# Later silu, later second halves of the streams, single-bank decays and another end of `up` in a two-layer trunk

## The chip, the cores and the metric

One core of one Trainium2 chip runs the whole program in one launch. The time is the device time of one execution in microseconds (us). Three executions of the kernel before took 2153.89, 2152.57 and 2152.16 us; their median is 2152.57.

## The reference

Two residual layers over 1024 tokens of width 1024, all in float32. Layer 0 mixes tokens with a gated MLP and with windowed attention; layer 1 with chunked gated linear attention (GLA). Each layer ends in a gated MLP with a causal convolution of width 3. The parts that the change touches:

```python
def gla_mixer(h, w_in, w_a2, b_a, head_g, w_out):
    z = h @ w_in
    q, k, v, r, ga = jnp.split(z, [hk, 2 * hk, 2 * hk + hv, 2 * hk + 2 * hv], axis=-1)
    log_a = jax.nn.log_sigmoid((ga @ w_a2 + b_a).astype(jnp.float32)) / C_TAU
    o = gla_chunked(heads(q, C_DK) * (C_DK ** -0.5), heads(k, C_DK), heads(v, C_DV), heads(log_a, C_DK))
    o = rms_norm(o, head_g)
    o = o.transpose(0, 2, 1, 3).reshape(Bn, S, hv) * jax.nn.silu(r.astype(jnp.float32))
    return o.astype(h.dtype) @ w_out

def conv_ffn(h, w_gate, w_up, conv_w, conv_b, w_down):
    g = causal_dwconv(h @ w_gate, conv_w, conv_b)
    return (jax.nn.silu(g) * (h @ w_up)) @ w_down
```

There are 4 GLA heads with 128 query and key columns and 256 value columns each; the MLP is 2816 wide.

## The kernel before

**Products.** TensorE multiplies float32 in a reduced form. So each operand is split into a high part (ScalarE's copy, line 100, a CAST in the profile) and a low part (VectorE's difference, line 101), and each product is three passes, `PASSES`: high x high, high x low, low x high. The third pass needs the low part of the weights.

**Streams.** The large products go by Strassen's scheme with seven half-size products instead of eight. A *stream* makes two 128-column blocks of an output for all 1024 tokens. Its `step(p)` splits the weights of product p (a raw quarter of the weights, or a sum of quarters: S5, S6, S7, S3), issues 12 matmuls of 128x512 (4 blocks x 3 passes) into a PSUM bank and then empties the bank or adds it to an output. Three banks serve a stream: A for product 2, C for 5 and 3, B for 1, 6, 7 and 4. Bank B is emptied between two products: 1 and 6 and 4 by a copy on ScalarE, 7 in the GLA by an addition on VectorE (`V.tensor_add(C22, C22, o)`, line 1063), in the MLP by a copy on ScalarE and an addition from there. C collects two products: the second is added to an output after both.

**GLA** (function `gla`). After the values (`values`, banks `pv`) come eight streams, q0 r0 q1 r1 ... r3: `q{h}` makes query and key of head h, `r{h}` its gate, which silu (line 1168) turns in place and which is stored to `rsd` for the first three heads. After each q comes `core(h)`: eight chunks of 128 tokens with small matmuls (`pat`, `pog`), then `decays(h + 1)`: two matmuls `pla`, then |x|, exp and ln on ScalarE (lines 1082 to 1085, two tables of functions), a difference on VectorE (line 1086), eight scans on VectorE (line 1089), a difference on GpSimd (line 1094) and exponentials. The first decays are made within `values`, in a wide slot (two banks) of the pool `mm`.

**Raw weights and sums.** A stream's two raw halves (`rq`, `rr`) come by DMA from SyncE's queue into four buffers; its sums have two buffers.

**The MLP.** `ffn_up` runs 22 streams, gate and up in turn (g0, u0, ... g20, u20), with bank names `pgA`, `puB` and so on; `ffn_down` comes after u20.

**What sets the order.** The kernel is written without waits: a scheduler with a timeline model of its own arranges each engine's instructions from the program and puts the waits in. Each engine takes its own queue in order. `tc.keep_in_program_order(ins)` holds an instruction at its place in the program; `tc.issue_after(ins)`, used by the change alone, makes VectorE's instructions that are written in the block come after `ins` on VectorE. PSUM has eight banks; after the values they are five for the tag `m1` and three for `pt`.

Of the kernel before, what the change touches and what calls it, by code (L numbers as in the profile page):

```python
# [55 lines left out]
def trunk(ctx: ExitStack, tc: tile.TileContext, a, out):  # L56
# [181 lines left out]
    def ffn_up(l, T3, ps, pool, norm_end):  # L238
# [6 lines left out]
        def stream(kind, f):  # L245

            raws = [load_raw(w_of(kind)[l, f + i], f"r{kind}{f + i}") for i in range(2 if f else 1)]
            A11, A12, A21, A22 = (raws[i][:, c] if f or not i else None for i in range(2) for _, c in HALVES)
            out = pool.tile([P, 2, S], F32, tag=kind, bufs=1, name=f"{kind}{f}")
            (C11, C12), (C21, C22) = ([out[:, i, c] for _, c in HALVES] for i in range(2))  # L250
            s1 = pool.tile([P, 512], F32, tag="s1", bufs=2, name=f"s1{kind}{f}")
            sums, bank, made = {}, {}, {}

            def summed(name, x, y, op):
                sums[name] = pool.tile([P, 512], F32, tag="S", bufs=4, name=f"{name}{kind}{f}")
                G.tensor_tensor(sums[name], x, y, op=op)  # L256
# [12 lines left out]

            def prep(p):  # L270
                if f == 0 and p > 2:
                    w = wp.tile([P, 2, 512], F32R, tag="w", name=f"w{kind}{f}p{p}")
                    Q.dma_start(f32(w), sided[l][kind, p])
                    made[p] = [w[:, i, :] for i in range(2)]
                else:
                    made[p] = parts_of(left(p), f"w{kind}{f}p{p}")

            def step(p):
                if p not in made:
                    prep(p)  # L280
                L = made[p]

                b = {2: "A", 5: "C", 3: "C"}.get(p, "B")
                more = b in bank
                if not more:
                    bank[b] = ps.tile([P, 512], F32, tag="pt" if b == "A" else "m1", name=f"p{kind}{b}{f}")
                o = bank[b]
                for j in range(4):
                    for ii, jj in PASSES:
                        T.matmul(o, L[ii][:, j * P : j * P + P], right[p][:, jj, j, :], skip_group_check=more,  # L290
                                 start=(not more and j == 0 and (ii, jj) == PASSES[0]),
                                 stop=(j == 3 and (ii, jj) == PASSES[-1]))
                if p == 1:
                    A.copy(s1, o)
                elif p == 2:
                    V.tensor_add(C11, s1, o)
                elif p == 6:
                    A.copy(C12, o)
                elif p == 5:
                    A.copy(C22, o)  # L300
                elif p == 7:
                    A.copy(s1, o)  # L302
                    V.tensor_add(C22, C22, s1)  # L303
                elif p == 4:
                    A.copy(C21, o)  # L305
                elif p == 3:
                    V.tensor_add(C12, C12, o)

            return step, out, prep
# [50 lines left out]
        for i, (kind, f) in enumerate(todo):  # L360
# [5 lines left out]
            if 0 < i < len(todo) - 1:  # L366
                nxt = stream(*todo[i + 1])
                nxt[0](1)
            step(4)
            step(3)  # L370
            if kind == "g":
                ts = conv(f, out)
            else:
# [524 lines left out]
    def gla(ps, narrow, gl, T3, rl):  # L898
# [43 lines left out]
        def values():  # L942

            for i, (col, step, w) in enumerate(((0, 272, 1), (256, 256, 2), (512, 512, 1))):
# [6 lines left out]
                for m in sorted(range(NT // (2 * w)), key=lambda m: 2 * w * m < 4):  # L951
# [26 lines left out]
                    if (i, m) == (1, 1):  # L978
                        decay_input()
                    if (i, m) == (2, 2):  # L980
                        first = decays(0, "mm")
            return first

        def minus(o, t, x, y):
# [32 lines left out]
        def stream(name, src, pool, **tag):  # L1017
# [24 lines left out]
            def step(p):  # L1042
# [17 lines left out]
                elif p == 5:  # L1060
                    A.copy(C22, o)
                elif p == 7:
                    V.tensor_add(C22, C22, o)
                elif p == 4:
                    A.copy(C21, o)
                elif p == 3:
                    V.tensor_add(C12, C12, o)
# [73 lines left out]
                return stream(f"q{h}", [a["w_qk"][2 * h + i] for i in range(2)], gl, tag="out", bufs=1)  # L1141
            return stream(f"r{h}", [a["w_r"][2 * h + i] for i in range(2)], rl, tag="r")

        cur = begin(*todo[0])
        cur[0](1)
        for i, (kind, h) in enumerate(todo):
            step, out = cur
            for p in (5, 6, 2, 7) if i + 1 < len(todo) else (6, 2, 7):
                step(p)
            if i + 1 < len(todo):  # L1150
                nxt = begin(*todo[i + 1])
                nxt[0](1)
            step(4)
            step(3)
            if i + 2 == len(todo):
                nxt[0](5)
            if kind == "q":
# [5 lines left out]
                core(h, out[:, 0, :], out[:, 1, :], dec)  # L1163
                if h + 1 < HEADS_C:
                    dc = decays(h + 1)
            else:
                for _, c in HALVES:
                    A.activation(out[:, :, c], out[:, :, c], AF.Silu)
                if h + 1 < HEADS_C:
                    Q.dma_start(rsd[:, 2 * h : 2 * h + 2, :], out)  # L1170
                else:
                    return ps, out
            cur = nxt


# [8 lines left out]

    def narrow():
        pss.close()
        return banks(pss, m1=5, pt=3)

    a_cat = even(gm_open)
    Q.dma_start(hg, a["head_g"])  # L1190
# [155 lines left out]
```

## Time and profile before

| of the profiled execution | |
|---|---|
| time of the execution | 2153.94 us |
| span from first to last instruction | 2152.2 us |
| TensorE (PE) busy | 2125.0 us, 99% |
| TensorE's weight loads (PEld) | 1801.6 us, 84% |
| VectorE (DVE) | 1528.2 us, 71% |
| ScalarE (ACT) | 1034.8 us, 48% |
| GpSimd (POOL) | 490.5 us, 23% |
| DMA queue of SyncE (q1), share of 16 engines | 48.3% |
| TensorE's idle time by waits, the longest | pj 5.9, po 2.2 in three, pBq 2.1 in two, pj 2.1, pv 1.6 us |

A row of the timeline gives the start in us from the span's beginning, the time from start to end, engine, line, operation, `out<-in`, shapes, and the count of equal instructions in the row; in square brackets the idle time of that engine just before it and what ended it. PE is TensorE's matmul, PEld its weight load, SPq the queue of DMAs. Names in the profile lose their last number (`pBq` is bank B of any q stream); `or` and `oq` are the outputs of r and q streams, `wq1p` the split weights of q1.

### The profile page before, as it was taken

The page shows a single profiled execution, that of the slowest core. Times are in us where ns is not written, and L with a number is a line of the kernel's source. Part 1 is how long each engine was busy: PE and PEld are TensorE (multiplying, and loading weights), DVE is VectorE, ACT ScalarE, POOL GpSimd, SP SyncE. Part 2 cuts the span into 40 slices and gives each one's busy share as a digit, 9 for nine tenths or more (in the row PEclk, how much of TensorE's full clock was granted, in tenths as well). Part 3 has the DMA queues.
Part 4 walks back from the last instruction along what each step waited for, and adds up shares of the span by engine and source line. Part 5 has one row for each costly group of instructions (what it writes and reads, how often), then busy time and mean ns, then how long its engine had stood idle before and what let it go on. Part 6 is the DMA issues. An engine that isn't in the chain of part 4 may idle for free.

```text
span 2152.2 us, 29720 instructions
## 1 busy us (share of the span) xinstructions
PE 2125.0 (99%) x10444; PEld 1801.6 (84%) x10444; DVE 1528.2 (71%) x2451; ACT 1034.8 (48%) x1998; POOL 490.5 (23%) x521
## 2 busy tenths in 40 slices
PE   8999999999999999999999999999999999999999
PEld 7999988888888888888898888878788888888887
DVE  7566655587878889655577777677778888785554
ACT  7555664264444444444454455535544444444443
POOL 6444310013424334000010011011234334220000
PEclk9999999999999999999999999999999999999999
DMA  7122313754444544765553233486554444457664
GB/s 273 33 68 68 104 43 115 262 196 156 153 164 154 174 154 150 258 230 198 208 179 108 79 106 100 138 291 213 176 166 161 166 154 155 162 181 280 214 216 165
DMA packets 159413, 353.70 MB, mean 164 GB/s; under 512 B 17392, under 2 KB 54256, under 8 KB 158880
## 3 DMA queue, kind: packets, MB, share of 16 engines
q1 hardware_dynamic: 159264, 351.81, 48.3%
q8 instruction: 82, 1.34, 0.3%
q14 instruction: 67, 0.55, 0.1%
HBM read 243.15 MB, written 108.59 MB: 163 GB/s over the span
## 4 chain that ended last, share of the span: by engine, by line
PE 91%; DVE 3%; DMA 2%; ACT 2%; issue 1%; SPq 0%; POOL 0%; DVEq 0%; ACTq 0%
PE puB L290 11%; PE pgB L290 11%; PE po L190 7%; PE pv L190 6%; PE pj L190 6%; PE pgC L290 6%; PE puC L290 6%; PE pdB L397 5%; PE pdC L397 5%; PE pdO L397 4%; PE puA L290 3%; PE pgA L290 3%; PE pdP L397 2%; PE pdQ L397 2%; PE pu L190 2%; PE pBq L1051 2%
## 5 line engine op out<-in xcount | busy, mean ns | idle before, releaser
L101 DVE TENSOR_TENSOR da<-ar,da 128x512 fp32r<-128x512 f32 x154 | 106.1, 689 | 154.7 <-ACT da L100 154.6
L100 ACT CAST da<-ar 128x512 fp32r<-128x512 f32 x154 | 95.9, 623 | 206.7 <-PE pdC L397 99.6
L190 PE MATMUL po<-wo,hq 128*128 128x512 f32 x768 | 184.6, 395 | 2.3 <-ACT hq L100 2.2
L190 PEld LDWEIGHTS po<-wo,hq 128*128 128x128 f32 x768 | 141.5, 188 | 32.6 <-ACT hq L100 2.9
L190 PE MATMUL pv<-wv,hq 128*128 128x512 f32 (+2 forms) x768 | 140.8, 340 | 1.6 <-DVE b L1083 1.6
L397 PE MATMUL pdB<-dw,da 128*128 128x512 f32 x528 | 135.5, 391 | 0.9 <-ACT u L305 0.7
L397 PE MATMUL pdC<-dw,da 128*128 128x512 f32 x528 | 135.1, 390 | 0.0
L190 PEld LDWEIGHTS pv<-wv,hq 128*128 128x128 f32 x768 | 118.7, 189 | 16.4 <-DVE b L1083 2.1
L397 PEld LDWEIGHTS pdB<-dw,da 128*128 128x128 f32 x528 | 98.7, 188 | 22.4 <-ACT u L305 1.1
L256 POOL TENSOR_TENSOR S1g<-rg 128x512 f32<-128x512 f32 x20 | 30.0, 1501 | 381.9 <-DMA wsd<-D 322.6
L397 PEld LDWEIGHTS pdC<-dw,da 128*128 128x128 f32 x528 | 99.0, 188 | 20.5
L101 DVE TENSOR_TENSOR dw<-wr,dw 128x512 fp32r<-128x512 f32 x154 | 105.7, 686 | 11.1 <-ACT dw L100 11.0
L140 POOL TENSOR_SCALAR rn<-ssq 128x1 f32<-128x1 f32 x24 | 9.7, 403 | 450.0 <-ACT h L148 245.1
L190 PE MATMUL pj<-wq,hq 128*128 128x384 f32 x576 | 110.2, 339 | 0.0
L100 ACT CAST dw<-wr 128x512 fp32r<-128x512 f32 x154 | 95.0, 617 | 16.2 <-DMA wr<-in_w_dn 9.3
L397 PE MATMUL pdO<-dw,da 128*128 128x512 f32 x396 | 102.2, 389 | 0.2 <-DVE dw L101 0.2
L190 PEld LDWEIGHTS pj<-wq,hq 128*128 128x128 f32 x576 | 99.1, 188 | 0.0
L397 PEld LDWEIGHTS pdO<-dw,da 128*128 128x128 f32 x396 | 74.3, 188 | 16.0 <-DVE dw L101 0.6
L319 DVE SCALAR_TENSOR_TENSOR t<-g,cw,t 128x1022 f32<-128x1022 f32 x44 | 76.6, 1742 | 0.1
L318 DVE SCALAR_TENSOR_TENSOR t<-g,cw,t 128x1023 f32<-128x1023 f32 x44 | 58.8, 1337 | 16.4 <-ACT t L317 16.4
L303 DVE TENSOR_TENSOR g<-g,s1g 128x512 f32<-128x512 f32 x22 | 15.2, 691 | 76.9 <-ACT s1g L302 76.9
L320 ACT ACTIVATE t<-t 128x1024 f32<-128x1024 f32 x44 | 46.7, 1062 | 32.2 <-DVE t L319 32.2
(1080 smaller groups left out, 5438.9 us busy)
## 6 DMA issues: line engine op xcount, KB each, us to landing
ar<-actd SPq DMA_DIRECT2D x70, 512.0 KB, 3.5
rd<-in_w_down SPq DMA_DIRECT2D x44, 512.0 KB, 3.6
wsd<-D SPq DMA_DIRECT2D x88, 256.0 KB, 2.2
rg<-in_w_gate SPq DMA_DIRECT2D x42, 512.0 KB, 3.7
ru<-in_w_up SPq DMA_DIRECT2D x42, 512.0 KB, 4.6
wr<-wsd SPq DMA_DIRECT2D x40, 512.0 KB, 4.4
actd<-t SPq DMA_DIRECT2D x66, 256.0 KB, 2.2
wr<-in_w_dn SPq DMA_DIRECT2D x30, 512.0 KB, 4.8
```

Source lines behind the costliest of these rows:

```text
L100: (hi or A.copy)(dst[0], src)
L101: (lo or V.tensor_sub)(dst[1], src, f32(dst[0]))
L140: G.tensor_scalar(r, ssq, 1.0 / n, EPS, op0=ALU.mult, op1=ALU.add)
L190: T.matmul(o, L[i], R[jj][:, sl], start=(k == 0 and (ii, jj) == PASSES[0]), stop=(k == nk - 1 and (ii, jj) == PASSES[-1]))
L256: G.tensor_tensor(sums[name], x, y, op=op)
L290: T.matmul(o, L[ii][:, j * P : j * P + P], right[p][:, jj, j, :], skip_group_check=more, start=(not more and j == 0 and (ii, jj) == PASSES ...
L303: V.tensor_add(C22, C22, s1)
L318: V.scalar_tensor_tensor(t[:, 1:], g[:, : S - 1], w(1), t[:, 1:], op0=ALU.mult, op1=ALU.add)
L319: V.scalar_tensor_tensor(t[:, 2:], g[:, : S - 2], w(0), t[:, 2:], op0=ALU.mult, op1=ALU.add)
L320: A.activation(t, t, AF.Silu)
L397: T.matmul(o, L[ii][:, t * P : t * P + P], R[jj], skip_group_check=more, start=start and not more and (ii, jj) == PASSES[0], stop=stop and ...
L1051: T.matmul(o, L[ii][:, j * P : j * P + P], right[p][:, jj, j, :], skip_group_check=more, start=(not more and j == 0 and (ii, jj) == PASSES ...
```

## The change

Five edits:

- In `ffn_up` the first and the last stream (g0, u20), in both layers, end with products 7, 3, 4 instead of 7, 4, 3. The first matmul of 3 is held there.
- The first decays are put into single banks (tag `pt`) instead of a slot of the wide pool.
- In the GLA the steps 4 and 3 of every stream are written under `issue_after` of product 7's addition: on VectorE their low parts, the sum S3 and the additions come behind it.
- Silu of `r{h}` and its store are written after product 6 of the next q stream instead of after the r stream, and held in the order of the program. For the last head they stay.
- `narrow()` opens the pool of `pt` ahead of that of `m1`, so that `pt` has other banks.

```diff
@@ ffn_up, step
-            def step(p):
+            def step(p, pin=False):
...
-                        T.matmul(o, L[ii][:, j * P : j * P + P], right[p][:, jj, j, :], skip_group_check=more,
...
+                        mm = T.matmul(o, L[ii][:, j * P : j * P + P], right[p][:, jj, j, :], skip_group_check=more,
...
+                        if pin and j == 0 and (ii, jj) == PASSES[0]:
+                            tc.keep_in_program_order(mm)
@@ ffn_up, the loop over streams
             if 0 < i < len(todo) - 1:
                 nxt = stream(*todo[i + 1])
                 nxt[0](1)
-            step(4)
-            step(3)
+                step(4)
+                step(3)
+            else:
+                step(3, pin=True)
+                step(4)
@@ gla, values
                     if (i, m) == (2, 2):
-                        first = decays(0, "mm")
+                        first = decays(0, "pt")
@@ gla, step
                 elif p == 7:
-                    V.tensor_add(C22, C22, o)
+                    return V.tensor_add(C22, C22, o)
@@ gla, the loop over streams
+        def gates(h, out):
+            for _, c in HALVES:
+                tc.keep_in_program_order(A.activation(out[:, :, c], out[:, :, c], AF.Silu))
+            if h + 1 < HEADS_C:
+                Q.dma_start(rsd[:, 2 * h : 2 * h + 2, :], out)
+
-        cur = begin(*todo[0])
+        cur, pending = begin(*todo[0]), None
...
             for p in (5, 6, 2, 7) if i + 1 < len(todo) else (6, 2, 7):
-                step(p)
+                added = step(p)
+                if p == 6 and pending:
+                    gates(*pending)
+                    pending = None
...
-            step(4)
-            step(3)
+            with tc.issue_after(added.ins):
+                step(4)
+                step(3)
...
+            elif h + 1 < HEADS_C:
+                pending = h, out
             else:
-                for _, c in HALVES:
-                    A.activation(out[:, :, c], out[:, :, c], AF.Silu)
-                if h + 1 < HEADS_C:
-                    Q.dma_start(rsd[:, 2 * h : 2 * h + 2, :], out)
-                else:
-                    return ps, out
+                gates(h, out)
+                return ps, out
@@ narrow
-        return banks(pss, m1=5, pt=3)
+        return banks(pss, pt=3, m1=5)
```

How the instructions stand on the engines, at three places. Here the names keep their numbers: `pBq0` is bank B of stream q0, `wq0p7` the weights of its product 7.

TensorE, from product 2 of q0 to the start of `core(0)`. Before:

```order
L1051 MATMUL pBq0_11606<-Tm1_10706,wq0p6_11641 128x512 x12
L1051 MATMUL pAq0_11660<-hq10_87,wq0p2_11657 128x512 x2
L1051 MATMUL pBr0_11701<-hq00_85,wr0p1_11698 128x512 x12
L1051 MATMUL pCq0_11625<-hq11_88,wq0p3_11733 128x512 x8
L1051 MATMUL pBq0_11606<-Tm2_10707,wq0p7_11676 128x512 x12
L1051 MATMUL pCq0_11625<-hq11_88,wq0p3_11733 128x512 x4
L1051 MATMUL pBr0_11701<-Tm1_10706,wr0p6_11978 128x512 x12
L1051 MATMUL pBq0_11606<-hq01_86,wq0p4_11715 128x512 x12
L1051 MATMUL pBr0_11701<-Tm2_10707,wr0p7_12013 128x512 x12
L1107 MATMUL pat00_11755<-oq0_11601 128x128
```

After:

```order
L1056 MATMUL pBq0_11606<-Tm1_10706,wq0p6_11641 128x512 x12
L1056 MATMUL pAq0_11660<-hq10_87,wq0p2_11657 128x512 x2
L1056 MATMUL pBr0_11701<-hq00_85,wr0p1_11698 128x512 x12
L1056 MATMUL pBq0_11606<-Tm2_10707,wq0p7_11676 128x512 x12
L1056 MATMUL pBq0_11606<-hq01_86,wq0p4_11715 128x512 x12
L1056 MATMUL pCq0_11625<-hq11_88,wq0p3_11733 128x512 x12
L1056 MATMUL pBr0_11701<-Tm1_10706,wr0p6_11978 128x512 x2
L1112 MATMUL pat00_11755<-oq0_11601 128x128
```

Between 7 and 4 of q0 stood `pCq0` and product 6 of r0; now 4 follows 7 without anything between, then 3, then two matmuls of r0's product 6.

TensorE, from the decays of head 1 (`pla10`, `pla11`) on, after `core(0)`. Before:

```order
L1079 MATMUL pla10_11931<-gaT_10730,wa2_10715 128x512
L1079 MATMUL pla11_11935<-gaT_10730,wa2_10715 128x512
L1051 MATMUL pAq1_12129<-hq10_87,wq1p2_12126 128x512
L1051 MATMUL pCr0_11962<-Tm0_10705,wr0p5_11959 128x512 x12
L1051 MATMUL pBq1_12038<-hq00_85,wq1p1_12035 128x512 x12
L1051 MATMUL pCq1_12094<-Tm0_10705,wq1p5_12091 128x512 x12
L1051 MATMUL pBr1_12170<-hq00_85,wr1p1_12167 128x512 x2
L1051 MATMUL pCr0_11962<-hq11_88,wr0p3_12070 128x512 x7
L1051 MATMUL pBr0_11701<-hq01_86,wr0p4_12052 128x512 x12
L1051 MATMUL pCr0_11962<-hq11_88,wr0p3_12070 128x512 x5
L1051 MATMUL pBq1_12038<-Tm1_10706,wq1p6_12110 128x512 x12
```

After:

```order
L1084 MATMUL pla10_11931<-gaT_10730,wa2_10715 128x512
L1084 MATMUL pla11_11935<-gaT_10730,wa2_10715 128x512
L1056 MATMUL pCr0_11962<-Tm0_10705,wr0p5_11959 128x512 x12
L1056 MATMUL pBq1_12038<-hq00_85,wq1p1_12035 128x512 x12
L1056 MATMUL pBr0_11701<-hq01_86,wr0p4_12052 128x512 x12
L1056 MATMUL pCr0_11962<-hq11_88,wr0p3_12070 128x512 x12
L1056 MATMUL pCq1_12091<-Tm0_10705,wq1p5_12088 128x512 x2
L1056 MATMUL pBq1_12038<-Tm1_10706,wq1p6_12107 128x512
L1056 MATMUL pCq1_12091<-Tm0_10705,wq1p5_12088 128x512 x10
L1056 MATMUL pBq1_12038<-Tm1_10706,wq1p6_12107 128x512
L1056 MATMUL pAq1_12129<-hq10_87,wq1p2_12126 128x512 x2
```

Products 4 and 3 of r0 now stand ahead of products 5, 6 and 2 of q1; before, 2 and 5 of q1 and a part of r1's 1 stood ahead of them.

VectorE at the same place, from the difference of the decays (`g11`) on. Before (product 4's and 3's low parts of r0 stand further up, ahead of `pla`):

```order
L1086 TENSOR_TENSOR g11_11929<-b1_11930,g11_11929 128x1024
L1063 TENSOR_TENSOR or0_11696<-or0_11696,pBr0_11701 128x512
L101 TENSOR_TENSOR wq1p4_12184<-rq11_12031,wq1p4_12184 128x512
L1089 SCALAR_TENSOR_TENSOR b1_11930<-one_10718,g11_11929 128x128 x8
L1057 TENSOR_TENSOR oq1_12033<-s1q1_12034,pAq1_12129 128x512
L101 TENSOR_TENSOR wq1p3_12202<-S3q1_12200,wq1p3_12202 128x512
L1091 TENSOR_TENSOR dec1_11950<-b1_11930 128x7
```

After:

```order
L1091 TENSOR_TENSOR g11_11929<-b1_11930,g11_11929 128x1024
L1068 TENSOR_TENSOR or0_11696<-or0_11696,pBr0_11701 128x512
L101 TENSOR_TENSOR wr0p4_12052<-rr01_11694,wr0p4_12052 128x512
L1033 TENSOR_TENSOR S3r0_12068<-rr00_11692,S6r0_11976 128x512
L1094 SCALAR_TENSOR_TENSOR b1_11930<-one_10718,g11_11929 128x128 x8
L1033 TENSOR_TENSOR S5q1_12086<-rq11_12031 128x512
L101 TENSOR_TENSOR wr0p3_12070<-S3r0_12068,wr0p3_12070 128x512
L1096 TENSOR_TENSOR dec1_11950<-b1_11930 128x7
L1033 TENSOR_TENSOR S6q1_12105<-S5q1_12086,rq10_12029 128x512
L1097 TENSOR_TENSOR dec1_11950<-dec1_11950,b1_11930 128x7
L101 TENSOR_TENSOR wq1p5_12088<-S5q1_12086,wq1p5_12088 128x512
```

The low parts of r0's products 4 and 3 and the sum S3r0 now stand behind the addition to `or0`, the last of them behind the scans and the first sum of q1; the low parts of q1's products come behind that.

More of the change, by code (lines that the diff above doesn't have):

```diff
@@ L289, in step @@
                     for ii, jj in PASSES:
-                        T.matmul(o, L[ii][:, j * P : j * P + P], right[p][:, jj, j, :], skip_group_check=more,
-                                 start=(not more and j == 0 and (ii, jj) == PASSES[0]),
-                                 stop=(j == 3 and (ii, jj) == PASSES[-1]))
+                        mm = T.matmul(o, L[ii][:, j * P : j * P + P], right[p][:, jj, j, :], skip_group_check=more,
+                                      start=(not more and j == 0 and (ii, jj) == PASSES[0]),
+                                      stop=(j == 3 and (ii, jj) == PASSES[-1]))
+                        if pin and j == 0 and (ii, jj) == PASSES[0]:
+                            tc.keep_in_program_order(mm)
                 if p == 1:
```

## The prediction

> **What bounds the kernel now.** I read the page first (busy shares, clock, chain), then the table by stage of the gated linear attention (GLA), then the timeline wherever TensorE's rows have an idle time.
>
> ```profile
> PE 2125.0 (99%) x10444; PEld 1801.6 (84%) x10444; DVE 1528.2 (71%) x2451; ACT 1034.8 (48%) x1998; POOL 490.5 (23%) x521
> ...
> PEclk9999999999999999999999999999999999999999
> ...
> PE 91%; DVE 3%; DMA 2%; ACT 2%; issue 1%; SPq 0%; POOL 0%; DVEq 0%; ACTq 0%
> ...
> 1202.60:1247.60 45.00, 45.00 (x212) 37.70 (x211) 31.23 (x63) 17.65 (x44) 4.94 (x14) 1.00 0.32 96
> 1247.60:1298.90 51.30, 51.30 (x238) 42.58 (x237) 37.30 (x75) 28.24 (x57) 7.78 (x18) 1.00 0.32 103
> 1298.90:1351.60 52.70, 51.64 (x238) 42.45 (x238) 37.29 (x75) 29.63 (x58) 7.76 (x18) 1.00 0.31 102
> 1351.60:1412.00 60.40, 59.26 (x281) 49.14 (x279) 39.25 (x80) 35.09 (x69) 8.60 (x20) 1.00 0.49 164
> ```
>
> TensorE is the bound: busy for 99% of the span, 91% of the chain, clock full. Within the four heads (the stage rows give length, then busy time of PE, PEld, DVE, ACT, POOL, then clock) it idles only 2.2 us in 209. The number of matmuls does not change, so the change is worth the waits that it takes from TensorE's queue, less those that it puts in.
>
> **What it removes.** The three kinds of wait, with the rows around them, and an undisturbed row of twelve matmuls (1221.88):
>
> ```profile
> 1167.82 0.63 PE L1079 MATMUL pla<-gaT,wa 96*128 96x512 f32 x2
> ...
> 1170.08 3.22 PE L190 MATMUL pv<-wv,hq 128*128 128x512 f32 x13 [1.62 <-DVE b L1083]
> ...
> 1221.88 2.88 PE L1051 MATMUL pBr<-Tm,wr0p 128*128 128x512 f32 x12
> ...
> 1321.33 1.05 ACT L1168 ACTIVATE or<-or 128x1024 f32<-128x1024 f32 x1
> ...
> 1322.29 0.56 ACT L1059 COPY oq<-pBq 128x512 f32<-128x512 f32 x1
> ...
> 1322.90 3.06 PE L1051 MATMUL pBq<-Tm,wq2p 128*128 128x512 f32 x12 [1.06 <-ACT oq L1059]
> ...
> PE pBq L1051 <- ACT oq L1059: 2.1, 2, 1.1
> ...
> 888.34 1.89 PE L290 MATMUL puB<-hq,wu20p 128*128 128x512 f32 x7 [0.68 <-ACT s1u L302]
> ...
> 1935.08 3.02 PE L290 MATMUL puB<-hq,wu20p 128*128 128x512 f32 x12 [0.68 <-ACT s1u L302]
> ...
> 1938.78 1.66 PE L397 MATMUL pdB<-dw,da 128*128 128x512 f32 x6 [0.68 <-ACT u L305]
> ```
>
> Twelve undisturbed matmuls are one row of 2.88 us, the last of which lasts 0.39: a pitch of 2.49 / 11 = 0.227 us. A wait so costs its idle time and the 0.16 by which a matmul's record outlasts the pitch; about 0.1 more goes where the row after it is stretched (3.02 or 3.06 for 2.88).
>
> - First decays in single banks: two `pla` banks replace a slot of the wide pool, for which the next `pv` waited until VectorE's L1083 had read it. 1.62 + 0.16, **-1.8**.
> - Silu put later: product 7 of `q2` and `q3` waits for ScalarE's copy of product 6, which stands behind silu's second half (1321.33, copy 1322.29). Two times 1.06 + 0.16 + 0.1, **-2.65**. Behind the later silu stand ScalarE's high part for product 3 and the next copies, which TensorE wants only 46 matmuls (10.4 us) after product 6 in the new order; cover enough for its load of a table and two halves (two halves of 1.05, and a load as long as those of the decays, below).
> - `up`'s end as 7, 3, 4: product 4 waited for the copy of product 7 out of the same bank; product 3 (another bank) now covers it. In layer 1 `pdB` also waited, for product 4's copy; it now waits for sums that are long done, and `pdC`, which waits for that copy, comes six matmuls (1.36 us) later, when the copy of 0.58 is over. One wait in layer 0, two in layer 1, each 0.68 + 0.16 + 0.1: **-2.85**. For the first `gate` stream, where the 7 stands in a like place, I see no such row and cost it at nothing, bounds -1 to +1.
>
> Removed: **7.3 us**. The bank swap changes no count and gets nothing, bounds -0.5 to +0.5; of the reordered start of layer 0's second output half I say the same, with a bound of 1.
>
> **What it adds at product 4 of each q.** Before, twelve or more matmuls of other products stood between 7 and 4 of such a stream:
>
> ```profile
> 1220.97 1.07 PE L1051 MATMUL pCq<-hq,wq0p 128*128 128x512 f32 x4
> ...
> 1221.17 0.69 DVE L1063 TENSOR_TENSOR oq<-oq,pBq 128x512 f32<-128x512 f32 x1 [2.62 <-PE pBq L1051]
> ...
> 1224.60 1.75 PE L1051 MATMUL pBq<-hq,wq0p 128*128 128x512 f32 x7
> ...
> 1275.09 0.68 DVE L1063 TENSOR_TENSOR oq<-oq,pBq 128x512 f32<-128x512 f32 x1
> ...
> 1275.69 0.68 DVE L101 TENSOR_TENSOR wr1p<-S3r,wr1p 128x512 fp32r<-128x512 f32 x1
> ```
>
> VectorE's L1063 empties product 7's bank (1221.17); the four `pCq` and the twelve `pBr` of 1221.88 hid it. In the new order 4 follows 7 directly, in that bank: end of the last matmul 0.39 after its start, 0.04 to L1063, 0.69, some 0.06 to start, against a pitch of 0.23: 0.95. Its third matmul needs the low part, which is now queued behind L1063: VectorE operations stand 0.60 apart (1275.09, 1275.69), which ends 1.76 after the last matmul's start, while the third would come at 1.62: 0.14 more. Four heads x 1.08 = **+4.3** (bounds 3.8 and 5).
>
> **What it adds between heads.** Three times, from head h to h+1, the new order puts TensorE's `pCr`, `pBq`, `pBr` (4), `pCr` (3) behind `pla`, and all `pAq` and `pCq` of the next head later, since their low parts stand behind the scans on VectorE. The rows of the first such change, and where the second differs:
>
> ```profile
> 1245.82 0.59 PE L1118 MATMUL pog<-v,ats 128*128 128x256 f32 x2
> ...
> 1247.62 0.82 PE L1079 MATMUL pla<-gaT,wa 96*128 96x512 f32 x2
> ...
> 1247.87 0.48 DVE L1131 TENSOR_SCALAR og<-pog,ro 128x256 f32<-128x256 f32 x1 [1.34 <-POOL ro L141]
> ...
> 1248.51 2.94 PE L1051 MATMUL pCr<-Tm,wr0p 128*128 128x512 f32 x12
> ...
> 1249.52 0.63 ACT L100 CAST wr1p<-rr 128x512 fp32r<-128x512 f32 x1
> ...
> 1250.03 1.07 ACT L1084 ACTIVATE g<-g 128x1024 f32<-128x1024 f32 x1
> ...
> 1251.12 1.28 ACT L1085 ACT_TABLE_LOAD   x1
> ...
> 1252.41 1.06 ACT L1085 ACTIVATE g<-g 128x1024 f32<-128x1024 f32 x1
> ...
> 1253.51 1.22 DVE L1086 TENSOR_TENSOR g<-b,g 128x1024 f32<-128x1024 f32 x1 [2.02 <-ACT g L1085]
> ...
> 1254.65 0.68 DVE L1063 TENSOR_TENSOR or<-or,pBr 128x512 f32<-128x512 f32 x1
> ...
> 1255.85 2.62 DVE L1089 TENSOR_TENSOR_SCAN b<-one,g 128x128 f32<-128x128 f32 x8
> ...
> 1258.62 1.92 POOL L1094 TENSOR_TENSOR g<-b 128x1024 f32<-128x1024 f32 x1 [9.23 <-DVE b L1089]
> ...
> 1258.97 2.11 DVE L101 TENSOR_TENSOR wq1p<-S3q,wq1p 128x512 fp32r<-128x512 f32 x1
> ...
> 1298.98 0.82 PE L1079 MATMUL pla<-gaT,wa 96*128 96x512 f32 x2
> ...
> 1301.52 1.28 ACT L1084 ACT_TABLE_LOAD   x1
> ...
> 1306.28 1.23 DVE L1086 TENSOR_TENSOR g<-b,g 128x1024 f32<-128x1024 f32 x1 [3.43 <-ACT g L1085]
> ...
> 10.30 3.50 PE L190 MATMUL pj<-wx,hq 128*128 128x384 f32 x10 [2.11 <-DVE hq L101]
> ...
> rr<-in_w_r SPq DMA_DIRECT2D x8, 512.0 KB, 3.7
> ```
>
> (The last two rows, an early wait and the loads of `r`'s weights, are for the rivals.)
>
> - Until product 4 of `r`. Its bank is emptied by L1063, which stands behind L1086. From `pla` to L1063's end was 1255.33 - 1247.62 = 7.7 us; the 0.5 us of the cast at 1249.52 leaves ScalarE's chain there: 7.2, and 0.06 to start. TensorE has two `pla` and 24 matmuls to do: 5.9. The wait is 1.35, and 0.15 for the low part: **1.5**. Part of it falls earlier, at `pCr`, which needs `pog`'s bank back (2.69 us from 1245.82 to 1248.51 in the old order), but that only moves it. In the second and third change of heads there is one more table load (1301.52): L1086 starts 7.3 after `pla` (1298.98) for 5.9, 1.4 later: **2.9** each.
> - At product 3 of `r`. The low part of its weights stands, on VectorE, after L1063, one low part, one sum, eight scans and a sum of the next head. From L1063's end: 1.12 until the scans, 2.62, then 0.60 and 0.68: 5.0. TensorE has 4's twelve matmuls and two of 3, and started 0.2 later: 3.4. The wait is 1.7 if nothing disturbs VectorE. But the POOL operation L1094 starts as the scans end, and beside it a VectorE operation of 0.69 took 2.11 (1258.97). With that 1.42 the wait is **3.1**. I take it, since the two operations after the scans both read SBUF alone, as the one in the row does; bounds 1.7, and 3.6 if the low part stands still for all of POOL's 1.92.
>
> Sum between heads: 1.5 + 2.9 + 2.9 + 3 x 3.1 = **+16.6** (12.4 to 18.1). What stands behind it on VectorE, the next head's low parts, comes late too, but twelve matmuls of product 3 lie ahead of each.
>
> [...]
>
> **Sum.** -7.3 + 4.3 + 16.6 = +13.6. The profiled execution took 2153.94 us (span 2152.2), so 2167.5; it lies 1.4 above the median of the runs, which makes **2166** on the median's footing.
>
> **Rivals.**
>
> 1. VectorE undisturbed at the scans (it finishes both operations before POOL takes hold): 1.7 for 3.1, so 2166 - 4.2 = **2162**. For it: the sum starts first. Against: the one row of the kind shows 2.11.
> 2. The waits between heads do not come, so the change is faster: **2149.6** (2152.6 - 7.3 + 4.3). One mechanism, at product 4 of `r`: if VectorE had taken L1063 and the two low parts ahead of L1086, the scans would stop nobody. It decides once the 7.2 us from `pla` fall under 5.9 and the 5.0 behind it under 3.4. For it: before, TensorE idled nowhere there. Against: VectorE takes its queue in order, and there L1086 stands first.
> 3. The clock falls. The waits at products 4 and 3 (up to 2.9, 3.1) lie 2.7 apart. If TensorE went on at half clock for the twelve matmuls behind each of three long waits, that is 3 x 2.72 more: **2174**. Against: after the 2.11 us that `pj` waits at 10.30 the clock row shows nothing.
> 4. The loads of `r`'s next weights come late: their buffers are now free only with the sum ahead of the scans, 8.4 us after `pla`. One landing time of 3.7 us, once: **2170**. Against: by the order they are wanted some 24 us after `pla`, twice that.
>
> [...]
>
> **Chances.** Forecast 0.48, undisturbed VectorE 0.27, no waits between heads 0.14, late loads 0.06, clock 0.05. This kernel's measurement tells about 0.2% (4.3 us) from no change: faster means below 2148.3, slower above 2156.9. Rival 2 falls on both sides of the first bound with its own spread of 2 us: 0.06 faster, 0.08 same. All others are slower: 0.86. The range, 2156 to 2171, takes the bounds of the sum (2161.5 to 2168.4, the first from 3.8 and 12.4) and rivals 1 and 4, and reaches below them half the way to rival 2, for waits between heads of half the size; it leaves out 2 and 3. The likeliest case alone: 2163 to 2169.
>
> **What would show it.** After: no idle row at `pv` behind `pla`, none at `pBq` 7 of `q2`, `q3`, none at `puB` and `pdB`; in their place four rows of `pBq` with 0.8 to 0.9 idle, released by VectorE's add, and in each head change idle times ahead of `pBr` and within `pCr`, about 4.6, 6.0 and 6.0 in sum, behind VectorE. If TensorE's idle time over the four heads stays under 8 us, the prediction is wrong in the head changes; if over 25, in what follows them.

## The result and the profile after

The changed kernel takes 2166.84 us in the median (2165.03 to 2169.53), the kernel before, run beside it, 2153.23: a ratio of 1.0054 with a 95% interval of 1.0044 to 1.0064. It is slower by 13.6 us. The profiled execution took 2169.53 us with a span of 2167.8, so it is the longest of the six.

The page of the changed kernel (busy time and share, TensorE's clock, the chain):

```profile
PE 2131.6 (98%) x10444; PEld 1805.8 (83%) x10444; DVE 1525.3 (70%) x2451; ACT 1037.0 (48%) x1998; POOL 495.9 (23%) x521
...
PEclk9999999999999999999999999999999999999999
...
PE 93%; DVE 3%; ACT 1%; DMA 1%; issue 1%; POOL 0%; SPq 0%; DVEq 0%; ACTq 0%
```

The counts are as before. Where the time went is read best from the starts of the same matmuls in the two traces. The table gives, for stretches between such marks, the time in the changed kernel less the time before, worked out from the starts in both traces:

| stretch, up to | before at | after at | difference of the stretch |
|---|---|---|---|
| the last gMLP matmul of layer 0 (`pm`) | 355.08 | 356.53 | +1.4 |
| `puC` of u2, layer 0 (second output half, start of the MLP) | 544.79 | 548.06 | +1.8 |
| `pgC` of g20, layer 0 | 868.47 | 871.74 | 0.0 |
| `pdO`, layer 0 (end of up, start of down) | 921.92 | 923.70 | -1.5 |
| the transposes `pgt` of the decays' input | 1144.79 | 1146.54 | 0.0 |
| first product of q0 (values, first decays) | 1202.83 | 1202.73 | -1.85 |
| last matmul of r3 (the GLA's streams) | 1408.01 | 1423.57 | +15.65 |
| `puC` of u2, layer 1 (output product, start of the MLP) | 1591.53 | 1609.03 | +1.9 |
| `pgC` of g20, layer 1 | 1915.20 | 1932.71 | 0.0 |
| `pdO`, layer 1 | 1968.83 | 1984.45 | -1.9 |
| the end | 2152.18 | 2167.80 | 0.0 |

One expectation below gives 2.8 for the row of layer 1's `puC`. It counts the GLA up to its last `pog` (1410.62 and 1425.31). Before, eight transposes `pc` of the output product, 0.9 us, stand ahead of that `pog`; in the changed kernel they stand behind it. Up to the last matmul of r3 every run has the same matmuls, so the text goes by that mark.

The waits that were to go are gone: the table of TensorE's waits over the GLA has no row with ScalarE's copy any more, over the two ends of `up` it has none at all, and `pv` follows `pla` without idle time. What is there now, over the GLA (engine, tile, line, what it waited for: us in total, times, longest):

```profile
PE pBq L1056 <- DVE oq L1068: 3.4, 4, 0.9
PE pBr L1056 <- DVE or L1068: 3.1, 3, 1.5
PE pCr L1056 <- DVE wr2p L101: 3.0, 1, 3.0
PE pCr L1056 <- DVE og L1136: 2.0, 3, 0.7
PE pCr L1056 <- DVE wr1p L101: 1.3, 1, 1.3
PE pCr L1056 <- DVE wr0p L101: 1.3, 1, 1.3
```

These are the four waits at product 4 of q and, three times each, `pCr` for `pog`'s bank, `pBr` for product 7's bank, and `pCr` within product 3 for its low part. The timeline of the first change of heads (start, length, engine, line, operation, shapes, idle time ahead and its end), with a q row ahead of it and the third change below:

```profile
1220.07 3.20 PE L1056 MATMUL pBq<-hq,wq0p 128*128 128x512 f32 x12 [0.85 <-DVE oq L1068]
...
1252.70 0.68 DVE L1068 TENSOR_TENSOR or<-or,pBr 128x512 f32<-128x512 f32 x1
...
1253.44 3.15 PE L1056 MATMUL pBr<-hq,wr0p 128*128 128x512 f32 x12 [0.17 <-DVE or L1068]
...
1254.51 2.63 DVE L1094 TENSOR_TENSOR_SCAN b<-one,g 128x128 f32<-128x128 f32 x8
...
1257.05 0.66 DVE L1033 TENSOR_TENSOR S5q<-rq 128x512 f32<-128x512 f32 x1
1257.28 2.85 POOL L1099 TENSOR_TENSOR g<-b 128x1024 f32<-128x1024 f32 x1 [9.41 <-ACT or L1070]
1257.63 0.68 DVE L101 TENSOR_TENSOR wr0p<-S3r,wr0p 128x512 fp32r<-128x512 f32 x1
...
1258.23 1.92 DVE L1096 TENSOR_TENSOR dec<-b 128x7 f32<-128x7 f32 x1
1258.37 2.57 PE L1056 MATMUL pCr<-hq,wr0p 128*128 128x512 f32 x10 [1.33 <-DVE wr0p L101]
...
1371.02 0.66 DVE L1033 TENSOR_TENSOR S5q<-rq 128x512 f32<-128x512 f32 x1
1371.24 2.21 POOL L1099 TENSOR_TENSOR g<-b 128x1024 f32<-128x1024 f32 x1 [10.69 <-ACT or L1070]
1371.60 2.40 DVE L101 TENSOR_TENSOR wr2p<-S3r,wr2p 128x512 fp32r<-128x512 f32 x1
...
1374.06 2.11 PE L1056 MATMUL pCr<-hq,wr2p 128*128 128x512 f32 x8 [3.01 <-DVE wr2p L101]
```

In the first change VectorE did the low part at 1257.63 in 0.68 us; GpSimd's L1099 lasted 2.85 instead of 1.92, and the next VectorE operation was the one to stand still (L1096, 1.92 for seven columns). In the third the low part itself took 2.40. The wait of product 3 is 1.33 idle in the one case and 3.01 in the other.

The +1.9 at the start of layer 1's MLP has another cause. The stretches around it, with length, busy time of PE, PEld, DVE, ACT and POOL, then the clock granted to TensorE; and the rows of TensorE:

```profile
1532.00:1536.00 4.00, 4.00 (x19) 3.33 (x18) 3.69 (x6) 3.13 (x6) 0.00 (x0) 1.00 0.97 374
1536.00:1540.00 4.00, 2.06 (x13) 1.42 (x11) 1.81 (x3) 0.88 (x3) 0.00 (x0) 1.00 0.64 195
1540.00:1543.00 3.00, 2.32 (x6) 1.82 (x6) 2.51 (x5) 3.00 (x11) 0.00 (x0) 0.50 0.40 161
1543.00:1546.00 3.00, 3.00 (x8) 2.31 (x7) 2.62 (x5) 1.57 (x3) 0.00 (x0) 0.50 0.00 0
```

```profile
1539.04 1.07 PE L162 MATMUL pt<-ident,xt 128*128 128x128 f32 x8 [1.95 <-issue]
1540.79 5.49 PE L290 MATMUL puA<-hq,wu0p 128*128 128x512 f32 x12 [0.68 <-DVE g L298]
```

At 1540.0, behind a wait of 1.95 and within the eight transposes that follow it, the clock fell from 1.00 to 0.50, and it stayed there for 6.8 us. A second profile of the same kernel (the last run but one below) has the twelve matmuls at full clock:

```profile
1544.15 3.01 PE L290 MATMUL puA<-hq,wu0p 128*128 128x512 f32 x12 [0.69 <-DVE g L298]
```

In the first profile they took 5.49 us instead of 3.01. From the start of the first of the twelve to that of the fifteenth matmul it is 6.10 us (1540.79 to 1546.89) instead of 3.31: 2.8 us, more than the whole difference of that stretch.

### The profile page after: what moved, and what is told of

Read it like the earlier page. It is cut to its first block, busy times and chain, and to the rows that moved or that the text cites. A ratio compares the mean times of both kernels' runs of the same rounds, so it can differ in the third digit from the quotient of the medians.

```text
span 2167.8 us, 29671 instructions
## 1 busy us (share of the span) xinstructions
PE 2131.6 (98%) x10444; PEld 1805.8 (83%) x10444; DVE 1525.3 (70%) x2451; ACT 1037.0 (48%) x1998; POOL 495.9 (23%) x521
## 4 chain that ended last, share of the span: by engine, by line
PE 93%; DVE 3%; ACT 1%; DMA 1%; issue 1%; POOL 0%; SPq 0%; DVEq 0%; ACTq 0%
PE puB L290 11%; PE pgB L290 11%; PE po L190 7%; PE pv L190 6%; PE pj L190 6%; PE pdB L402 6%; PE pgC L290 6%; PE puC L290 6%; PE pdC L402 5%; PE pdO L402 4%; PE puA L290 3%; PE pgA L290 3%; PE pdP L402 2%; PE pdQ L402 2%; PE pu L190 2%; PE pBq L1056 2%
## 5 line engine op out<-in xcount | busy, mean ns | idle before, releaser
L256 POOL TENSOR_TENSOR S4u<-ru,S2u 128x512 f32<-128x512 f32 x20 | 48.9, 2444 | 54.6 <-DVE wg2p L101 9.7
```

## The experiments

The first three take the order on VectorE away stream by stream.

**The order kept for the r streams alone.**

```diff
-            with tc.issue_after(added.ins):
+            with tc.issue_after(added.ins) if kind == "r" else ExitStack():
```

> The change with the order on VectorE (issue after product 7's addition) kept for the r streams alone; the q streams take products 4 and 3 as the scheduler likes. Theory: the four waits of 4 behind 7 go, some 1.2 us each (1.01 and two of 0.11 in the changed kernel), the head changes stay: 2166.8 - 5 = about 2162, the rows of pBr and pCr idle as before. Rival, that the head changes wait because the next head's weights are split late on whatever account, gives the same here; the rival that the q order itself holds up the head change gives 2150 to 2155.

Measured: 2165.1 us, ratio to before 1.0050 (1.0036 to 1.0064). The head changes stay as expected, and the four q waits are gone. But the GLA became shorter by 3.7 only (+11.9 against before, where the whole change has +15.65), and 1.7 of that is the third low part, which did not meet GpSimd in this execution. A new wait stands elsewhere:

```profile
PE pBr L1056 <- DVE or L1068: 3.1, 3, 1.4
PE pCr L1056 <- DVE og L1136: 2.0, 3, 0.7
PE pBr L1056 <- ACT or L1064: 1.9, 2, 0.9
```

The third row is product 7 of r1 and r2 waiting for the copy of their product 6. So part of the 5 us of the q streams comes back at another place; the time's interval does not tell 2165 from the changed kernel.

**The order kept for the q streams alone.**

```diff
-            with tc.issue_after(added.ins):
+            with tc.issue_after(added.ins) if kind == "q" else ExitStack():
```

> The change with that order kept for the q streams alone. Theory: the four waits at product 4 of q stay (0.85 us idle each), and the waits at pCr, pBr and pCr in the head changes (13.4 us by the traces) go, as r's low parts come ahead of the difference and the scans again: 2166.8 - 13.4 = about 2153.5. Rival (late silu and late loads hold up the head changes): over 2160, with pBr or pCr still idle.

Measured: 2157.9 us, ratio 1.0016 (1.0007 to 1.0026); the GLA has +4.7 against before, 11.0 less than with the whole change. Every wait of the head changes is gone, the four q waits stay, and `core` got three short ones (`pat`), 2 us with the gaps around them; the time is 4.4 above the expected one:

```profile
PE pBq L1056 <- DVE oq L1068: 3.4, 4, 0.9
PE pat L1112 <- DVE st L1129: 1.5, 3, 0.5
```

The rival (late silu or late loads hold up the head change) falls: both are as in the changed kernel.

**Without the order on any stream.**

```diff
-            with tc.issue_after(added.ins):
-                step(4)
-                step(3)
+            step(4)
+            step(3)
```

> The change without that order on any stream; the other four edits stay. Theory: both additions go, 2166.8 - 18.4 = about 2148.5, faster than before by 4 to 5; less than the 7.3 of the removed waits, as the changed kernel also lost 2 to 4 us where the MLP of each layer starts. Rival (the loss is silu's new place or the banks): still slower than before, above 2156.

Measured: 2152.72 us, ratio 0.9993 (0.9984 to 1.0002). The GLA is 1.65 shorter than before, the ends of `up` by 1.1 and 1.95, the values by 1.85; but the starts of the two MLPs cost +3.9 and +2.0. The rival falls, since it is not slower. The gain is 4 less than forecast: the GLA gave 17.3 of the expected 18.4, and the +3.9 holds 3.4 us at half clock (471.29 to 474.70, behind a wait of 2.82); the rest is not accounted for.

**Three edits alone:** first decays in single banks, silu late, 7, 3, 4 at the end of the last stream.

```diff
-                        first = decays(0, "mm")
+                        first = decays(0, "pt")
...
+            if i == len(todo) - 1:
+                step(3, pin=True)
+                step(4)
+            else:
+                step(4)
+                step(3)
...
+                if p == 6 and pending:
+                    gates(*pending)
+                    pending = None
```

> The kernel before with three of the edits only: first decays in single banks, silu put later, and 7, 3, 4 at the end of the last up stream alone (not the first gate stream); banks and VectorE's order as before. Theory: the 7.3 us of the removed waits and nothing else, 2153.2 - 7.3 = about 2146, ratio 0.9966. Rival (the scheduler or the later silu gives part of it back): 2149 to 2153.

Measured: 2153.92 us, ratio 0.9996 (0.9987 to 1.0005): nothing gained. Values -1.85, but the GLA +0.4, and of the two waits at the end of layer 1's `up` one stays. The rows of the GLA, then of the end of `up`:

```profile
PE pCq L1057 <- ACT vend L973: 1.7, 1, 1.7
PE pBq L1057 <- DVE oq L1069: 1.2, 1, 1.2
...
PE pdB L403 <- ACT u L307: 0.7, 1, 0.7
```

**The same three edits with the banks swapped for the GLA's pool alone.** No engine's order changes against the run before, only the banks.

```diff
-        return banks(pss, m1=5, pt=3)
+        return banks(pss, pt=3, m1=5) if swap else banks(pss, m1=5, pt=3)
```

(`gla` calls `narrow(True)`, layer 0 `narrow()`.)

> The same three edits as in the run of three edits, with the bank swap added for the GLA's pool alone (layer 0 keeps its banks). Every engine's order is the same as in that run; only the banks differ. Theory: the wait of 1.7 us that the first product 5 of q0 took there, for the copy of the last value tile, is gone, since its bank is no longer one of those of that tile: GLA shorter by 1.9, 2 us faster than the run of three edits. Rival (that wait came of ScalarE's order, not of the banks): the same wait and the same time.

Measured: 2152.17 us against 2155.24 of before, ratio 0.9986 (0.9977 to 0.9995). `pCq`'s wait for `vend` and `pdB`'s for `u` are both gone; the GLA is 2.0 shorter than in the run before, the end of `up` 1.0. So the bank swap was not idle: with the decays out of the wide pool, the last value tile stands in other banks, and without the swap the first C bank of q0 is one of them; and `pdB`'s first banks are those of `puA` instead of the one that product 4 fills. (Which banks these are is read from the kernel's pools; the profile does not name them. And it is the rows that tell the two runs apart: the intervals of their times overlap.)

**First decays in single banks alone.**

```diff
-                        first = decays(0, "mm")
+                        first = decays(0, "pt")
```

> The kernel before with one edit, the first decays in single banks. Theory of the prediction: the wait of pv behind pla goes, -1.8, nothing else: 2151.4. Theory after the run of three edits: -1.85 ahead of q0's product 1 and +1.9 at q0's product 5, which now waits for the last value tile's copy: 2153.2, no change.

Measured: 2155.42 us, ratio 1.0003 (0.9994 to 1.0012). -1.85 ahead of q0, +2.0 in the GLA, by this row:

```profile
PE pCq L1051 <- ACT vend L967: 1.8, 1, 1.8
```

The second theory holds: alone, this edit only moves its wait.

**The bank swap alone, in both layers.**

```diff
-        return banks(pss, m1=5, pt=3)
+        return banks(pss, pt=3, m1=5)
```

> The kernel before with the bank swap alone, in both layers. Theory: it moves layer 0's second output half and the start of its MLP in the scheduler's order, +1.8 at the MLP's start of layer 0 as in the changed kernel, nothing in the GLA: 2155. Rival (the changed end of the first gate stream made the 1.8): no change, 2153.2.

Measured: 2154.59 us, ratio 0.9999 (0.9990 to 1.0008). The trace shows +1.7 up to the start of layer 0's MLP and 0 in the GLA, as forecast, and -0.7 and -0.6 at the ends of `up`. Over all runs, that stretch of layer 0 has +1.2 to +3.9 in the seven profiles with the swap in layer 0, and -0.2 to +0.4 in five of the six without; the sixth, decays alone, has +1.7 with no edit there. So the swap in layer 0 most likely costs a microsecond or two, through the order that the scheduler makes of it, but one execution alone does not show it.

**7, 3, 4 at the end of the first gate stream alone.**

```diff
+            if i == 0:
+                step(3, pin=True)
+                step(4)
```

> The kernel before with 7, 3, 4 at the end of the first gate stream alone, in both layers. Theory: the start of the MLP in layer 1 loses some 2 us as it did in the changed kernel (2.8) and in the run without the order on VectorE (2.0), layer 0 nothing: 2155. Rival (those 2 us come from what precedes, layer 1's output product): no change within 1 us.

Measured: 2154.83 us, ratio 0.9998 (0.9989 to 1.0007), no loss in either layer (-0.2 and -1.0 at the MLPs' starts). The theory falls: the +1.9 of layer 1 does not come from this edit.

**Product 3 of the r streams alone set free.**

```diff
             with tc.issue_after(added.ins):
                 step(4)
+            with tc.issue_after(added.ins) if kind == "q" else ExitStack():
                 step(3)
```

> The changed kernel with product 3 of the r streams alone set free on VectorE (their product 4 and all of the q streams stay behind product 7's addition). Theory: it is the sum S3r, kept behind the difference of the decays, that holds the two buffers of sums and with them the next head's weights; free, it lets products 2 and 5 of the next q stand ahead of 4 and 3 of r again in TensorE's order, and all waits of the head changes go, the one at product 4 too: GLA shorter by about 10 us than in the changed kernel, as with the order kept for the q streams alone, so 2157. Rival (each wait has its own cause): only the wait within pCr goes (1.5, 1.5 and 3.2), 2166.8 - 6.2 = 2160.5, and pBr still waits for L1068.

Measured: 2154.14 us, ratio 0.9997 (0.9988 to 1.0007). The GLA is at +1.5 against before, 14.2 shorter than in the changed kernel, and the table of waits from q0 into the output product has two rows, of which `po` belongs to the output product:

```profile
PE pBq L1056 <- DVE oq L1068: 3.8, 4, 1.2
PE po L190 <- ACT hq L100: 0.3, 1, 0.3
```

The rival falls. The wait at product 4 is gone too, though L1068 and product 4's low part still stand behind the difference of the decays on VectorE: with the sum S3r and product 3's low part ahead of them, the end of product 2 and eleven matmuls of product 5 of the next q, and seven of r's own product 3, stand ahead of 4 again in TensorE's order, and cover it. So the whole loss of the head changes comes of holding back one sum and one low part; which of the two would do it alone was not tried. The time is 3 us below the expected one; the `pat` waits of the run for q alone are not there.

**Silu late alone.**

```diff
+            elif h + 1 < HEADS_C:
+                pending = h, out
```

(with `gates` after product 6, as in the change)

> The kernel before with silu put later and nothing else. Theory: the two waits of 7 for product 6's copy go (-2.45 in the GLA), and one of about 1.4 comes where product 4 of q2 follows 7's addition, as in the run without the order on VectorE: net -1.1, 2152 to 2153. Rival (the prediction's term): -2.65.

Measured: 2155.01 us, ratio 1.0002 (0.9992 to 1.0012). The GLA is 1.6 shorter: the two waits for the copy are gone, one of 1.2 for VectorE's addition is there, as the theory said. But the start of the output product lost 2.35 in this execution. The largest of its waits there, and then the only one of the kernel before:

```profile
PE pc L442 <- DMA cat<-ogd: 2.4, 3, 1.5
```

```profile
PE po L190 <- ACT hq L100: 1.2, 2, 1.0
```

With silu late in an otherwise unordered GLA, the output tiles of the heads (`cat`) arrive after TensorE wants them. The same row stands in the three other runs with late silu and without any order on VectorE (2.2, 1.1 and 0.6 us), but with 0.4 also in the run with the decays alone. Why they are later was not followed.

**The changed kernel again.**

> The changed kernel once more, for a second profile of it. [...] Rival: the half clock belongs to the change, and comes again.

Measured: 2167.84 us, ratio 1.0061 (1.0046 to 1.0076). The stretch up to the start of layer 1's MLP is at -1.7 now, so the +1.9 there belonged to one execution. Half clock came again, but in the GLA, where it makes +18.4 out of +15.65. Stretches as above, around the second head change, and TensorE's rows:

```profile
1312.00:1315.00 3.00, 3.00 (x13) 2.27 (x13) 3.00 (x9) 0.63 (x2) 0.00 (x0) 1.00 0.47 141
1315.00:1318.20 3.20, 0.41 (x2) 0.00 (x0) 3.20 (x4) 1.20 (x2) 2.21 (x1) 0.92 0.60 201
1318.20:1321.00 2.80, 2.56 (x6) 2.08 (x7) 2.80 (x7) 1.84 (x3) 0.00 (x0) 0.50 0.00 0
1321.00:1324.00 3.00, 3.00 (x8) 2.32 (x8) 1.58 (x4) 2.99 (x6) 0.00 (x0) 0.50 0.00 0
```

```profile
1311.79 3.16 PE L1056 MATMUL pBr<-hq,wr1p 128*128 128x512 f32 x12 [1.45 <-DVE or L1068]
1314.79 0.61 PE L1056 MATMUL pCr<-hq,wr1p 128*128 128x512 f32 x2
1318.44 4.63 PE L1056 MATMUL pCr<-hq,wr1p 128*128 128x512 f32 x10 [3.03 <-DVE wr1p L101]
```

Ten matmuls behind the wait of 3.03 took 4.63 us, those behind the wait of 1.33 in the first profile 2.57. Thirteen went at half pace: from the first to the fourteenth start 5.71 us (1318.44 to 1324.15), against 3.08 behind the wait of 3.01 in the first profile, so 2.6 us. This time it was the second change that met GpSimd; the first and third had 1.3.

**Decays in single banks, the end of the last stream, banks swapped for the GLA; silu where it was.**

```diff
-            elif h + 1 < HEADS_C:
-                pending = h, out
```

(against the run of three edits with swapped banks, with all of silu's edit taken out)

> The kernel before with the first decays in single banks, 7, 3, 4 at the end of the last up stream and the bank swap for the GLA's pool; silu where it was. Theory: what silu's new place gives in the GLA (1.6) it gives back at the start of layer 1's output product, where the tiles of the last head then arrive late (cat, 2.4 us of waits with silu late, none before), so that leaving it out costs nothing: -1.85 and 2 to 3 at the two ends of up, ratio 0.998. Rival: 1.6 slower than with silu late, ratio 0.9993.

Measured: 2149.87 us against 2156.27 of before beside it, ratio 0.9977 (0.9967 to 0.9988). This version beats both kernels, though by less than the two medians say: six executions of it with a granted clock of 1.000 took 2149.4 us in the mean, five such of before 2152.5, and eight of the seventeen of before stood at 0.998. Its interval overlaps with that of the same version with late silu (0.9977 to 0.9995), so which of those two is better stays open. The GLA is level, the ends of `up` -1.45 and -1.95, the values -1.85, the output product and the start of layer 1's MLP -2.5, a stretch that had -1.7 with the decays alone. Of TensorE's waits from the first decays to that start these are the largest:

```profile
PE pBq L1057 <- ACT oq L1065: 2.1, 2, 1.1
PE puA L290 <- DVE g L298: 0.7, 1, 0.7
```

## Why the prediction was right, and where it was not

The forecast of 2166 met 2166.84, with the sign, the place and the cause. The terms, against the two profiles of the changed kernel and the runs:

- *Removed waits, -7.3.* Decays -1.8: -1.85 measured. `up` -2.85: -1.9 in layer 1 as forecast, -0.9 to -1.5 in layer 0 for 0.95. Silu -2.65: its two waits are gone, so the step holds in the changed kernel. Alone it is worth 1.6 in the GLA and nothing in the whole.
- *The bank swap, "gets nothing".* This step failed, and its bounds of 0.5 with it. The swap is what keeps the decays' 1.85 and one of the two 0.95 of layer 1's `up`: without it the same order of instructions is 2.0 and 1.0 longer there (in the runs of three edits; from the changed kernel itself it was not taken out). The prediction read the waits of the kernel before and did not ask which banks the tiles would take next. The sum of the removed waits was right, the edits it was put down to were not; and in layer 0 the swap likely takes a microsecond or two.
- *Product 4 of q, +4.3.* Idle 0.85 each, and two more gaps of 0.11 within the twelve: 1.24 x 4 = 5.0, at the upper bound of 5. The run with the order for r alone shows that taking them away shortens the GLA by only 3.7, of which 1.7 is a low part that did not meet GpSimd.
- *Head changes, product 4: 1.5, 2.9, 2.9.* By the gaps between starts, of which `pog`'s bank makes 0.95: 1.5, 2.8, 2.8, within 0.1 of the forecast.
- *Head changes, product 3: 3.1 each.* This is the mis-sized term: 1.6, 1.6 and 3.3 in the first profile, 1.6, 3.3 and 1.6 in the second (idle 1.33 or 3.03 and the gaps around). The prediction took the stretched operation for every head and gave 0.27 to rival 1, in which VectorE comes through; the runs show both, one in three stretched in either profile of the change, none in that of r alone. The sum of the head changes is 13.7 for 16.6.
- *Rival 3, the clock,* had 0.05 and came, though not as a rule: once in the GLA of the second profile, 2.6 us, and once at the start of the MLP in the first, 2.8 us; both times the clock stood at 0.50 for 6.8 us. In the third head change of the first profile the same 3.01 idle left the clock at 1.00. A price of 2.72 was set for each of three head changes; at most one of them paid it. That such waits would bring half clock was the author's supposition. And the row against this rival was misread: the ten `pj` behind the wait at 10.30 start 0.32 us apart and the ones after them 0.17, so they ran at half pace. The profile has no record of the clock before 13.59 us, and its row shows full speed there.
- *Rivals 2 and 4.* The waits between heads came, and no load was late: neither a `rr` nor a `rq` stands among TensorE's waits.

So the GLA's +15.65 is 2.6 under the +18.2 of the forecast (4.3 + 16.6 - 2.65): product 3 gave 2.8 less, product 4 of q 0.7 more. That the total still meets is in part chance: in the first profile the named terms come to +10.4 (15.65 - 1.85 - 1.5 - 1.9) instead of 13.6; starts of the MLP and stretches at half clock, which the sum did not hold, filled it up. The forecast was right to within the bounds of its main terms, not to 0.84 us.

What the mechanism comes down to was also sharper than the prediction's telling. It named all of r's late low parts; the run with product 3 set free shows that S3r and product 3's low part do it without the others.

## What to carry to other kernels

Where TensorE is full and the instruction order is made by a scheduler, read for a constraint on one engine what it pushes back *behind* the held instruction: here two held VectorE operations of 0.69 us each took away the matmuls that covered a chain of 7 us, three times. A buffer moved to another pool can change the banks of what comes after it, so a wait that is gone from one row has to be looked for at the next tile in those banks; edits that look idle may hold up the gain of another. And two edits whose waits were real, the decays and silu, gave nothing when run alone, so a version is to be made from runs, not from a list of removed waits.

## What the runs showed of the hardware

- GpSimd and VectorE took turns for a whole operation in these rows: in the first head change GpSimd's 1.92 became 2.85, ending just as VectorE's next one, of seven columns, ended after 1.92; in the third VectorE's 0.69 became 2.40, ending 0.55 after GpSimd's. The kernel before has one like the third: the low part at 1258.97 took 2.11 and ended 0.54 after GpSimd's L1094 (1260.54). Which of them gave way changed between heads and executions of one program (the wait for the low part is 3.01 in the third change of the first profile, 3.03 in the second change of the second). The recorded starts do not tell whose turn it is: GpSimd's record begins at 1257.28, 0.35 ahead of the low part's, and the low part still ran first. The prediction's upper bound of 3.6 has the low part stand still for all of GpSimd's 1.92; here the first sum's turn was followed by the low part's in two of three cases.
- TensorE's granted clock fell to 0.50 for 6.8 us within a wait of 3.03 (second profile), and in another place after a wait of 1.95, within eight small transposes (first profile); at a wait of 3.01 elsewhere in the first profile it stayed at 1.00. By length the two waits of 3 us are alike: from the start of the last matmul ahead of it to the next start it is 3.4 us for both.
- What differs is where they lie. In the first profile the clock stood at 0.50 from 51.79 to 55.21, 3.413 us, and from 1540.00 to 1546.83, and these four times lie whole multiples of 3.413 us apart; so do those of the second profile (51.34, 58.17, 1317.69 and 1324.52). Between 60 us and the end of the program the clock fell four times in the fourteen profiles: at 1540.00 and 1317.69 in the two of the changed kernel, without the order on any stream (0.99 in the mean from 330 to 550 us) and with the order for q alone (0.99 from 1410 to 1550 us). At 1540.00 and 1317.69 it fell at the end of a stretch of this grid in which matmuls cover 1.47 and 1.13 us of the 3.41; in the first profile the least they cover in a stretch after which it stayed at 1.00 is 1.71. The wait of 3.03 lay for the most part in one such stretch (first row, second profile); the wait of 3.01 was shared by two (the other rows, first profile):

```profile
1314.28:1317.69 3.41, 1.13 (x5) 0.59 (x4) 3.41 (x6) 1.20 (x2) 2.06 (x1) 1.00 0.75 263
```

```profile
1369.34:1372.75 3.41, 1.71 (x8) 1.07 (x6) 3.41 (x8) 1.20 (x2) 1.51 (x1) 1.00 0.74 296
1372.75:1376.17 3.42, 2.12 (x9) 1.78 (x10) 3.41 (x7) 1.40 (x3) 0.70 (x1) 1.00 0.02 5
```

- The clock also falls early in the program, between 51 and 59 us, for 3.4 or 6.8 us, in eight of the fourteen profiles, with the same matmuls there in all of them; in the first profile of the changed kernel it fell at the end of a stretch of the grid in which matmuls cover 2.20 us. The stretch from 51 to 55 us, in the second profile of the changed kernel and in that of the decays alone:

```profile
51.00:54.70 3.70, 3.39 (x19) 3.39 (x18) 2.04 (x8) 2.04 (x7) 1.85 (x5) 0.55 0.34 115
```

```profile
51.00:54.70 3.70, 3.70 (x30) 3.70 (x30) 3.38 (x10) 2.69 (x10) 2.15 (x5) 1.00 0.20 66
```

The differences between profiles up to the last gMLP matmul (-1.25 to +3.5 against before) go with it: +1.4 or more in the eight, +0.7 or less in the others. Of the 96 executions of the kernel before that ran beside the experiments, the 45 with a mean granted clock of 1.000 took 2153.4 us in the mean, the 22 with 0.998 took 2156.6. A part of the spread between executions of one kernel is so explained, and the differences of 1 or 2 us between single profiles above are to be read with that in mind.
